# 64-byte operand starts, a start without GpSimd, output weights through gate buffers, and the first FFN weights between two norms

## The chip, the cores and the metric

The kernel runs on one core of a Trainium2 chip, in one launch, on one token sequence of 1024 positions with a model width of 1024. The time is the device time of one execution in microseconds (us), the median of the runs. PE is TensorE, DVE is VectorE, ACT is ScalarE, POOL is GpSimd and SP is SyncE, which issues the transfers.

## The reference, cut to what matters

```python
h = rmsnorm(x, norm_mix_pre)
q_a, f_a, i_a, g_a, q_b, k_b, v_b, gate_raw = split(h @ w_in)
y_a = hgrn2_mix(q_a, f_a, i_a, g_a, lb, hg_out_norm)         # 4 heads of 128, chunks of 64
y_b = diff_attention(q_b, k_b, v_b, lam, lam_init, da_subln)  # 4 heads, two softmaxes each
gate_a, gate_b = split(sigmoid(gate_raw))
merged = gate_a * (y_a @ w_up_a) + gate_b * (y_b @ w_up_b)
x = x + rmsnorm(merged @ w_out, norm_mix_post)
h = rmsnorm(x, norm_ffn_pre)
ff = silu(h @ w_ffn_gate) * (h @ w_ffn_up)                    # width 2816
x = x + rmsnorm(ff @ w_ffn_down, norm_ffn_post)
```

Everything is in float32; x is 1024 x 1024.

## The kernel before, in words

**Split operands.** Each float32 operand of a large product is cut into a high and a low half, and a product of two such operands is three matmuls (high with high, high with low, low with high) into one PSUM bank. The high half is a copy or cast on ACT, the low half a subtraction on DVE or POOL (`split`, L633 to L635). A matmul takes 128 rows by 512 columns.

**Stages.** (1) The input, transposed, arrives in eight tiles `xr`; ACT and DVE cut each into `act` halves (L270, L271), while PE begins the first two projections, `f0` and `q0`, tile by tile as they come. The weights of the projections come through `w_raw`, `w_hi` and `w_lo`, three buffers each (`fetch_w`, `split_w`); the constant `ON_DVE` says for which weights DVE makes the low half (L110), POOL makes the others. The squares of the input for the first norm (L284 on POOL for the first three tiles, L286 on ACT for the others) are summed on DVE, and `column_rstd` makes the statistics from them. (2) Four HGRN heads, then four attention heads, each woven with the remaining projections as filler: before a head, `next(filler)` puts a few steps of a gate projection (six matmuls each) on PE; then the head's first scores (L547) follow, whose operands `atw` DVE makes. (3) The up-projection: for each of eight column blocks j, two products with L143, L144 and L146, whose banks DVE multiplies by the gates (L741), adds (L745) and splits. `put_wo` (L718) brings the eight output weights through `w_raw` and splits them: two within the loop over j, on POOL, six behind it, on DVE and POOL in turn. (4) The out-projection (`out_mults`, L850 to L852) in eight row tiles t, with the two norms of `residual` (L798 to L809) behind each, and, `LAG` ticks later, the transposes of `transposed` (L832), which `put_T` (L816 to L820) splits into the FFN's left-hand tiles T. (5) The FFN's gate and up products, 22 units of seven products of 12 matmuls (`GateUp.product`, L950 to L953), each unit's weights loaded by `load_raw` (L887) and cut by `prep` into `hl` or slot tiles; the first two products of four units (`EARLY`) come first, then the rest. (6) `Down` (L1103 to L1106), and the last rows.

**What sets the order.** The program is written stage by stage; the builder's scheduler places the instructions on each engine within their dependencies, and each engine runs its row in order. `after` adds an ordering edge without a wait between engines. A `Ring` hands out buffers in turn; a `Cutter` cuts them from 16 KB slots.

**Where tiles lie.** The constants and the slots lie from the left end of the on-chip memory; the pools with `side="right"` (`wp`, `actp`, `gwp`, two slots and `hl_more`) lie from the right end. Counted from the sizes of the pools, every tile of the right side that PE reads starts at an odd multiple of 32 bytes, and every one of the left at a multiple of 64. T4 lies in a slot of the right side, the other T on the left.

Two places of the code that the rest speaks of:

```python
(dve if len(ws) in ON_DVE else pool).tensor_tensor(out=lo, in0=raw, in1=hi.bitcast(F32), op=ALU.subtract)
...
for _ in range(7):
    next(filler)
weave(attn(h, vs[2 + h // 2], (h % 2) * P), filler, AT_RATIO[h])
...
prepare(min(x + (1 if x < 2 * EARLY else AHEAD), len(seq) + 1))
```

## Time and profile before

| | |
|---|---|
| runs before | 1532.06, 1530.64, 1531.58 us; median 1531.58 |
| the profiled execution | 1532.58 us, of which the span of its records is 1530.7 |
| granted clock of PE, mean | 0.992 |
| PE busy | 1499.1 us of the span |
| DVE, ACT, POOL busy | 884.3, 604.8, 528.3 us |
| transfers | 189.44 MB, mean 124 GB/s |

The profile is of one execution. Busy times of the engines lie beside one another; a granted clock of 1.00 means that PE ran at its full 2.4 GHz, and the other level, 1.2 GHz, pulls the mean of a stretch below that. A matmul's duration in a record is longer than its distance to the next, since they are pipelined; the pace is the distance between two starts. "Idle before" in a row is time in which that engine had nothing running ahead of the instruction, with the instruction that released it.

### The profile page before, as it was taken

To read this page: it belongs to the slowest core of one execution; us is meant where nothing else is said; L and a number is where in the kernel's file an instruction comes from. 1 tells how busy PE (TensorE), PEld (TensorE's weight loads), DVE (VectorE), ACT (ScalarE), POOL (GpSimd) and SP (SyncE) were. 2 spreads that over 40 slices of the span, in tenths; PEclk is the share of its full clock that TensorE was granted. 3 is DMA by queue.
4 is the path that set the end of the run, shared out by engine and by line. 5 is a ranking of instruction groups with operands and counts; after the bars stand their busy time and mean duration, and the time that the engine had idled before them with its cause. 6 is when DMAs were issued, how large, how long until landed. Compare 5 with 4: busy or idle time off the path is not lost. (4 is left out here: it accounts for less than half of the span.)

```text
span 1530.7 us, 19524 instructions
## 1 busy us (share of the span) xinstructions
PE 1499.1 (98%) x7334; PEld 1255.9 (82%) x7334; DVE 884.3 (58%) x1596; ACT 604.8 (40%) x1138; POOL 528.3 (35%) x347
## 2 busy tenths in 40 slices
PE   8999999999999999999999999999999999999998
PEld 6988988989878888888877778888888888888886
DVE  8667387354474646554325777555555544477744
ACT  5422323225344343554325554444444444423211
POOL 4211111231221313124601265455555444456600
PEclk9999999999999999999999999999999999999999
DMA  5101021021121211174323336444444435977333
GB/s 218 56 28 55 15 70 42 31 81 41 56 69 56 69 70 55 56 287 159 117 85 122 110 98 241 157 152 151 151 151 149 146 109 191 377 283 259 138 130 118
DMA packets 53231, 189.44 MB, mean 124 GB/s; under 512 B 6032, under 2 KB 6160, under 8 KB 53136
## 3 DMA queue, kind: packets, MB, share of 16 engines
q1 hardware_dynamic: 53136, 188.18, 34.4%
q8 instruction: 58, 0.95, 0.2%
q14 instruction: 37, 0.30, 0.1%
HBM read 131.54 MB, written 56.62 MB: 123 GB/s over the span
## 5 line engine op out<-in xcount | busy, mean ns | idle before, releaser
L635 POOL TENSOR_TENSOR slot<-slot 128x512 fp32r<-128x512 f32 x166 | 228.7, 1388 | 190.6 <-ACT slot L634 190.0
L110 POOL TENSOR_TENSOR w_lo<-w_raw,w_hi 128x1024 fp32r<-128x1024 f32 x50 | 123.1, 2464 | 479.5 <-ACT w_hi L108 458.5
L634 ACT CAST slot<-slot 128x512 fp32r<-128x512 f32 x252 | 151.3, 620 | 227.9 <-PE mbank L952 48.8
L143 PE MATMUL gbank<-act,w_hi 128*128 128x512 f32 x560 | 225.7, 403 | 1.6 <-ACT act L270 1.5
L144 PE MATMUL gbank<-act,w_hi 128*128 128x512 f32 x560 | 220.8, 394 | 3.9 <-DVE act L271 3.9
L906 DVE TENSOR_TENSOR slot<-slot 128x512 f32<-128x512 f32 x120 | 107.1, 895 | 143.8 <-POOL slot L635 87.5
L146 PE MATMUL gbank<-act,w_lo 128*128 128x512 f32 x560 | 175.2, 392 | 0.0
L635 POOL TENSOR_TENSOR hl<-slot,hl 128x512 fp32r<-128x512 f32 x70 | 96.8, 1389 | 97.4 <-ACT hl L634 96.8
L144 PEld LDWEIGHTS gbank<-act,w_hi 128*128 128x128 f32 x560 | 105.5, 188 | 23.9 <-DVE act L271 4.9
L146 PEld LDWEIGHTS gbank<-act,w_lo 128*128 128x128 f32 x560 | 105.4, 188 | 22.6
L143 PEld LDWEIGHTS gbank<-act,w_hi 128*128 128x128 f32 x560 | 105.3, 188 | 21.4 <-ACT act L270 2.1
L108 ACT CAST w_hi<-w_raw 128x1024 fp32r<-128x1024 f32 x52 | 54.5, 1047 | 121.9 <-issue 68.7
L950 PE MATMUL gbank<-slot 128*128 128x512 f32 x232 | 92.2, 397 | 3.0 <-ACT slot L634 3.0
L953 PE MATMUL gbank<-slot 128*128 128x512 f32 x232 | 91.9, 396 | 0.6 <-POOL slot L635 0.6
L952 PE MATMUL gbank<-slot 128*128 128x512 f32 x232 | 91.9, 396 | 0.0
L558 ACT ACTIVATE s<-s,nm 128x128 f32<-128x128 f32 (+7 forms) x64 | 49.2, 769 | 86.0 <-DVE nm L556 86.0
L634 ACT CAST hl<-slot 128x512 fp32r<-128x512 f32 x70 | 43.3, 621 | 90.1 <-PE mbank L952 24.0
L237 PE MATMUL gbank<-w_hi,act 128*128 128x256 f32 x256 | 73.8, 288 | 0.0
L238 PE MATMUL gbank<-w_lo,act 128*128 128x256 f32 x256 | 72.8, 284 | 0.0
L239 PE MATMUL gbank<-w_hi,act 128*128 128x256 f32 x256 | 72.7, 284 | 0.0
L950 PE MATMUL mbank<-slot 128*128 128x512 f32 x176 | 69.2, 393 | 2.4 <-ACT slot L957 2.4
L953 PE MATMUL mbank<-slot 128*128 128x512 f32 x176 | 69.3, 394 | 0.0
(261 smaller groups left out, 3489.3 us busy)
## 6 DMA issues: line engine op xcount, KB each, us to landing
t<-slot SPq DMA_DIRECT2D x68, 512.0 KB, 3.3
slot<-t SPq DMA_DIRECT2D x68, 512.0 KB, 6.7
slot<-w_gu SPq DMA_DIRECT2D x48, 512.0 KB, 4.1
w_raw<-w_proj SPq DMA_DIRECT2D x36, 512.0 KB, 3.6
slot<-w_down SPq DMA_DIRECT2D x22, 512.0 KB, 4.8
g<-gw SPq DMA_DIRECT2D x16, 512.0 KB, 2.6
slot<-g SPq DMA_DIRECT2D x16, 512.0 KB, 4.7
xr<-xT SPq DMA_DIRECT2D x8, 512.0 KB, 8.2
```

What stands on the lines that cost most here:

```text
L110: (dve if len(ws) in ON_DVE else pool).tensor_tensor(out=lo, in0=raw, in1=hi.bitcast(F32), op=ALU.subtract)
L143: pe.matmul(ps, lhsT=hi[:, kw, :], rhs=rhs(ka, b, 0), start=first and i == 0, stop=False)
L144: pe.matmul(ps, lhsT=hi[:, kw, :], rhs=rhs(ka, b, 1), start=False, stop=False)
L146: pe.matmul(ps, lhsT=lo[:, kw, :], rhs=rhs(ka, b, 0), start=False, stop=last and i == n - 1)
L237: pe.matmul(ps[:, :256], lhsT=a[:, 0, :], rhs=hi[:, kt % 4, :], start=kt == 0, stop=False)
L238: pe.matmul(ps[:, :256], lhsT=a[:, 0, :], rhs=lo[:, kt % 4, :], start=False, stop=False)
L634: copied = act.copy(out=dst[:, 0], in_=src)
L635: eng.tensor_tensor(out=dst[:, 1], in0=src, in1=dst.bitcast(F32)[:, 0], op=ALU.subtract)
L906: dve.tensor_tensor(out=t, in0=a, in1=b, op=op)
L950: pe.matmul(ps, lhsT=hl[:, 0, w], rhs=t[:, 0, c, :], start=not on and c == 0, stop=False, skip_group_check=on)
L952: pe.matmul(ps, lhsT=hl[:, 0, w], rhs=t[:, 1, c, :], start=False, stop=False, skip_group_check=on)
L953: pe.matmul(ps, lhsT=hl[:, 1, w], rhs=t[:, 0, c, :], start=False, stop=c == 3, skip_group_check=on)
```

## The change

Five things, in the order of the program:

1. A tile of 32 bytes (`pad`) is put at the right end, so that every pool of the right side moves by 32 bytes.
2. While the input is split, POOL gets no work: the low half of weight 0 goes to DVE (`ON_DVE` with 0), and all eight squares go to ACT, behind its splits.
3. Before each attention head eight instead of seven steps of the filler are put on PE.
4. `put_wo` takes its raw buffer from the `tmp` ring, in which the gates were, and copies with ACT; the low halves on DVE from the third weight on come behind the last merged branch (`m_last`).
5. `residual` is a generator that stops between its two norms. Unit 0 is prepared behind row tile 6, unit 1 between the two norms of row tile 7; the out-projection's code stands behind the units for that. The lag of the transposes is one tick shorter from t = 4 on. `put_T` reads the copy in SBUF and not the bank. `prep` splits on DVE until product 16, then on POOL, and in the first eight products it is called one product earlier.

```diff
@@ -42,7 +42,7 @@
 PAIRS = 2 * CHUNKS
 ROWS = range(2 * PAIRS, NF)
 STEPS = (2, 8, 32)
-ON_DVE = (1, 4)
+ON_DVE = (0, 1, 4)
 NMASK = 1 + 3 * len(STEPS)
 HG_YIELD = (3, 2, 3)
 V_PRE, V_HG, V_DA, V_LB = 0, 8, 9, 10
@@ -56,6 +56,7 @@
 
     const = ctx.enter_context(tc.tile_pool(name="const", bufs=1))
     small = ctx.enter_context(tc.tile_pool(name="small", bufs=3))
+    ctx.enter_context(tc.tile_pool(name="pad", bufs=1, side="right")).tile([P, 8], F32, name="pad")
     old = ctx.enter_context(ExitStack())
     wp = old.enter_context(tc.tile_pool(name="wp", bufs=3, side="right"))
     hts = ctx.enter_context(ExitStack())
@@ -280,10 +281,7 @@
             next(f0)
             next(q0)
             sq = sqs if kt == 0 else start.tile([P, S], F32, name="sq", bufs=3)
-            if kt < 3:
-                pool.tensor_tensor(out=sq, in0=xrs[kt], in1=xrs[kt], op=ALU.mult)
-            else:
-                after(act.activation(out=sq, in_=xrs[kt], func=AF.Square), h_last, "the squares follow the splits")
+            after(act.activation(out=sq, in_=xrs[kt], func=AF.Square), h_last, "the squares follow the splits")
             if kt:
                 after(dve.tensor_tensor(out=sqs, in0=sqs, in1=sq, op=ALU.add), l_last, "the squares follow the splits")
         run(f0)
@@ -691,7 +689,7 @@
         if h + 1 < NH:
             todo.append(project(13 + h, partial(put_q, h + 1)))
         filler = chain(*todo)
-        for _ in range(7):
+        for _ in range(KT):
             next(filler)
         weave(attn(h, vs[2 + h // 2], (h % 2) * P), filler, AT_RATIO[h])
         if h + 1 == NH:
@@ -716,10 +714,13 @@
     wo = []
 
     def put_wo(eng):
-        raw = wp.tile([P, 1024], F32, name="w_raw")
+        raw = tmp.take()
         sp.dma_start(out=raw, in_=w_out[len(wo)])
         t = two(w_cut.take())
-        split(t, raw, eng)
+        act.copy(out=t[:, 0], in_=raw)
+        lo = eng.tensor_tensor(out=t[:, 1], in0=raw, in1=t.bitcast(F32)[:, 0], op=ALU.subtract)
+        if len(wo) >= WO_AHEAD and eng is dve:
+            after(lo, m_last, "the merged branches go first")
         wo.append(t)
 
     up_a = [(k, k) for k in range(4)]
@@ -744,7 +745,9 @@
             cs = slice(n * HALF, (n + 1) * HALF)
             dve.tensor_tensor(out=gs[0][:, cs], in0=gs[0][:, cs], in1=gs[1][:, cs], op=ALU.add)
             t = two(m_cuts[n].take())
-            split(t, gs[0][:, cs], dve if j == KT - 1 else pool)
+            act.copy(out=t[:, 0], in_=gs[0][:, cs])
+            m_last = (dve if j == KT - 1 else pool).tensor_tensor(out=t[:, 1], in0=gs[0][:, cs],
+                                                                  in1=t.bitcast(F32)[:, 0], op=ALU.subtract)
             row.append(t)
         mT.append(row)
         if j >= KT - WO_AHEAD:
@@ -798,6 +801,7 @@
             act.activation(out=h[:, cs], in_=ps, func=AF.Square, scale=1.0 / 32.0, accum_out=ss[:, d:d + 1])
             dve.tensor_tensor(out=ag[:, cs], in0=ps, in1=gpost[:, cs], op=ALU.mult)
         r = rstd(ss)
+        yield
         dve.scalar_tensor_tensor(out=x, in0=ag, scalar=r, in1=x, op0=ALU.mult, op1=ALU.add)
         sp.dma_start(out=x2_dram[t], in_=x)
         s2 = small.tile([P, 1], F32, name="ss1")
@@ -812,12 +816,12 @@
     def four(a):
         return a.rearrange("p (k c) -> p k c", c=P)
 
-    def put_T(i, b, src, eng, lo_src=None):
+    def put_T(i, b, src, eng):
 
         blk = slice(b * P, (b + 1) * P)
         t = T[i]
         act.copy(out=t[:, 0, :, blk], in_=four(src))
-        eng.tensor_tensor(out=t[:, 1, :, blk], in0=four(src if lo_src is None else lo_src),
+        eng.tensor_tensor(out=t[:, 1, :, blk], in0=four(src),
                           in1=t.bitcast(F32)[:, 0, :, blk], op=ALU.subtract)
 
     def transposed(t):
@@ -834,7 +838,7 @@
         if t < 4:
             for g, pt in enumerate(pts):
                 act.copy(out=f[:, g, :], in_=pt)
-                put_T(1 + g, b, f[:, g, :], dve, pt)
+                put_T(1 + g, b, f[:, g, :], dve)
             return
         a = fs[b]
         act.copy(out=f[:, 1, :], in_=pts[1])
@@ -860,26 +864,8 @@
         while due and due[0][1] <= 0:
             transposed(due.pop(0)[0])
 
-    load_x(0)
-    load_x(1)
...
-        residual(t, ps)
-        load_x(t + 2)
-        due.append([t, LAG])
-
-
+
+    prep_eng = [dve]
     raw_ring, hl_ring, sum_ring = Ring([raw0]), Ring([hl_more.tile([P, S], F32, name="hl") for _ in range(2)]), Ring([])
 
     def load_raw(src, ring=raw_ring):
@@ -925,7 +911,7 @@
             else:
                 src = self.sum(q(0, 1), self.s[6], ALU.subtract)
             t = two(hl_ring.take())
-            split(t, src)
+            split(t, src, prep_eng[0])
             self.hl[i] = t
 
     t2_dram = [[dram.tile([P, 2, HALF], F32, name=f"t2_{p}_{i}") for i in range(8)] for p in range(NF // 2)]
@@ -1005,15 +991,39 @@
         yield
 
     units = [GateUp(f) for f in range(NF)]
-    units[0].prep(1)
-    units[0].prep(2)
-    for i in (6, 3, 7):
-        new_T(i, 0)
...
+    load_x(0)
+    load_x(1)
...
+        rest = residual(t, ps)
+        next(rest)
+        if t == 7:
+            for i in (6, 3, 7):
+                new_T(i, 0)
+            raw_ring.parts = cuts(slot(1), S)
+            hl_ring.parts += cuts(slot(1), S)
+            mixed = slot(1)
+            sum_ring.parts = cuts(mixed, HALF, 0, 3 * HALF)
+            ev.parts = cuts(mixed, HALF, 3 * HALF) + cuts(slot(2), HALF)
+            units[1].prep(1)
+            units[1].prep(2)
+        run(rest)
+        load_x(t + 2)
+        due.append([t, LAG - (t >= 4)])
+        if t == 6:
+            units[0].prep(1)
+            units[0].prep(2)
 
     def late_T():
         while due:
@@ -1064,7 +1074,9 @@
             unit.prep(i)
 
     for x, (u, i) in enumerate(seq):
-        prepare(min(x + (1 if x < 2 * EARLY else AHEAD), len(seq) + 1))
+        prepare(min(x + (2 if x < 2 * EARLY else AHEAD), len(seq) + 1))
+        if x == 4 * EARLY:
+            prep_eng[0] = pool
         if x < 2 * EARLY and i == 2:
             units[u].raw = [None, None]
         if side and next(side[0], "end") == "end":
```

What this does to the order, at three places. First PE, at the first attention head: `act` are the input's halves, `atw` the operands of the scores, `gbank` the gate projection's banks. Before:

```order
L146 MATMUL gbank_2811<-act_190,w_lo_2736 128x512
L146 MATMUL gbank_2812<-act_193,w_lo_2736 128x512
L547 MATMUL mbank_2860<-atw_2793,atw_2728 128x256
L547 MATMUL mbank_2860<-atw_2794,atw_2728 128x256
L547 MATMUL mbank_2870<-atw_2799,atw_2731 128x256
L547 MATMUL mbank_2870<-atw_2800,atw_2731 128x256
L143 MATMUL gbank_2811<-act_198,w_hi_2734 128x512
L144 MATMUL gbank_2811<-act_198,w_hi_2734 128x512
L143 MATMUL gbank_2812<-act_201,w_hi_2734 128x512
L144 MATMUL gbank_2812<-act_201,w_hi_2734 128x512
```

and after the change:

```order
L147 MATMUL gbank_2815<-act_194,w_lo_2740 128x512
L147 MATMUL gbank_2816<-act_197,w_lo_2740 128x512
L144 MATMUL gbank_2815<-act_202,w_hi_2738 128x512
L145 MATMUL gbank_2815<-act_202,w_hi_2738 128x512
L144 MATMUL gbank_2816<-act_205,w_hi_2738 128x512
L145 MATMUL gbank_2816<-act_205,w_hi_2738 128x512
L147 MATMUL gbank_2815<-act_202,w_lo_2740 128x512
L147 MATMUL gbank_2816<-act_205,w_lo_2740 128x512
L545 MATMUL mbank_2874<-atw_2797,atw_2732 128x256
L545 MATMUL mbank_2874<-atw_2798,atw_2732 128x256
L545 MATMUL mbank_2884<-atw_2803,atw_2735 128x256
L545 MATMUL mbank_2884<-atw_2804,atw_2735 128x256
```

The six matmuls of the last input tile, which stood behind the four score matmuls, now stand ahead of them.

Second DVE, where the up-projection ends: L741 (L742 after) are the multiplies of banks by gates, L635 of 128x1024 (L721 after) the low halves of output weights. Before:

```order
L745 TENSOR_TENSOR slot_5873<-slot_5873 128x512 x2
L635 TENSOR_TENSOR slot_6606<-w_raw_6609,slot_6606 128x1024
L741 TENSOR_TENSOR slot_5873<-slot_5873,gbank_6529 128x512
L741 TENSOR_TENSOR slot_5873<-slot_5873,gbank_6530 128x512
L635 TENSOR_TENSOR slot_6615<-w_raw_6618,slot_6615 128x1024
L741 TENSOR_TENSOR slot_5873<-slot_5873,gbank_6557 128x512
L741 TENSOR_TENSOR slot_5873<-slot_5873,gbank_6558 128x512
L745 TENSOR_TENSOR slot_5873<-slot_5873 128x512 x2
L635 TENSOR_TENSOR slot_6371<-slot_5873,slot_6371 128x512
L635 TENSOR_TENSOR slot_6375<-slot_5873,slot_6375 128x512
```

and after the change:

```order
L746 TENSOR_TENSOR slot_5883<-slot_5883 128x512 x2
L742 TENSOR_TENSOR slot_5883<-slot_5883,gbank_6532 128x512
L742 TENSOR_TENSOR slot_5883<-slot_5883,gbank_6533 128x512
L742 TENSOR_TENSOR slot_5882<-slot_5882,gbank_6560 128x512
L742 TENSOR_TENSOR slot_5882<-slot_5882,gbank_6561 128x512
L746 TENSOR_TENSOR slot_5883<-slot_5883,slot_5882 128x512 x2
L749 TENSOR_TENSOR slot_6375<-slot_5883,slot_6375 128x512
L749 TENSOR_TENSOR slot_6379<-slot_5883,slot_6379 128x512
L721 TENSOR_TENSOR slot_6598<-slot_5882,slot_6598 128x1024
L721 TENSOR_TENSOR slot_6605<-slot_5883,slot_6605 128x1024
L721 TENSOR_TENSOR slot_6612<-slot_5883,slot_6612 128x1024
```

The weights' low halves stood between the multiplies; now they stand behind the merged branches' halves (L749).

Third ACT, at the start of the FFN: L804 and L809 (L808 and L813 after) are the second norm of row tile 7, L634 (L632 after) the casts of FFN weights, L819 (L823 after) those of T. Before:

```order
L819 CAST slot_7426<-slot_7116 128x4x128
L819 CAST slot_7424<-slot_6862 128x4x128
L957 COPY slot_7429<-gbank_7431 128x512
L819 CAST slot_7426<-slot_7116 128x4x128
L804 ACTIVATE slot_6640,ss1_7320<-slot_6639 128x1024
L634 CAST slot_7428<-slot_7427 128x512
L960 ACT_TABLE_LOAD
L960 ACTIVATE slot_7429<-slot_7429 128x512
L809 ACTIVATE slot_6639<-slot_6639,r1_7325 128x512 x2
L634 CAST slot_7428<-slot_7427 128x512
```

and after the change:

```order
L823 CAST slot_7409<-slot_6948 128x4x128
L632 CAST slot_7413<-slot_7412 128x512 x2
L823 CAST slot_7409<-slot_6948 128x4x128
L823 CAST slot_7410<-slot_7190 128x4x128 x2
L844 COPY slot_7190<-mbank_7376 128x512
L823 CAST slot_7048<-slot_7190 128x4x128
L632 CAST slot_7413<-slot_7412 128x512 x2
L801 ACTIVATE slot_6635,ss2_7400<-gbank_7333 128x512
L823 CAST slot_7409<-slot_6948 128x4x128
L801 ACTIVATE slot_6635,ss2_7400<-mbank_7334 128x512
```

The casts of the weights stood behind the last second norm (L804, L809); now four of them stand ahead of the row tile's first norm (L801).

## Rows read from the trace of the kernel before

**Rows 1.** The page: busy time of each engine (us, share of the span, instructions).

```profile
PE 1499.1 (98%) x7334; PEld 1255.9 (82%) x7334; DVE 884.3 (58%) x1596; ACT 604.8 (40%) x1138; POOL 528.3 (35%) x347
```

**Rows 2.** Stretches: us, PE, PEld, DVE, ACT, POOL busy (count), PEclk, DMA share, GB/s.

```profile
20.00:35.00 15.00, 15.00 (x68) 12.43 (x67) 14.80 (x18) 5.40 (x6) 2.73 (x1) 1.00 0.27 90
690.00:750.00 60.00, 60.00 (x258) 48.24 (x257) 23.02 (x34) 26.42 (x32) 31.01 (x19) 1.00 0.41 142
764.00:775.00 11.00, 8.79 (x32) 6.74 (x31) 4.92 (x7) 2.27 (x3) 0.28 (x1) 0.84 0.65 239
815.00:830.00 15.00, 12.86 (x53) 10.09 (x52) 8.95 (x13) 10.63 (x21) 1.62 (x3) 0.89 0.34 120
866.00:910.00 44.00, 38.01 (x152) 29.74 (x151) 33.87 (x40) 26.49 (x48) 28.25 (x20) 0.88 0.32 108
```

**Rows 3.** Timeline of PE in Down: start us, us, operation, count, idle before.

```profile
1308.87 0.40 PE L1103 MATMUL mbank<-hl,slot 128*128 128x512 f32 x1
...
1314.48 0.40 PE L1103 MATMUL gbank<-slot 128*128 128x512 f32 x1
...
1325.40 0.40 PE L1103 MATMUL gbank<-hl,slot 128*128 128x512 f32 x1
```

**Rows 4.** Groups by line: busy us, mean ns, idle before (PE, mixed pairs).

```profile
L143 PE MATMUL gbank<-slot,w_hi 128*128 128x512 f32 x128 | 50.7, 396 | 0.0
...
L950 PE MATMUL gbank<-slot,hl 128*128 128x512 f32 x120 | 47.3, 394 | 0.0
...
L950 PE MATMUL mbank<-slot,hl 128*128 128x512 f32 x88 | 34.9, 397 | 0.0
...
L1103 PE MATMUL gbank<-hl,slot 128*128 128x512 f32 x40 | 15.8, 394 | 0.0
...
L1103 PE MATMUL mbank<-hl,slot 128*128 128x512 f32 x32 | 12.6, 394 | 0.0
```

**Rows 5.** Timeline of DVE while the input is split.

```profile
7.13 4.24 DVE L271 SCALAR_TENSOR_TENSOR act<-xr,vec,act 128x512 fp32r<-128x512 f32 x2 [3.42 <-ACT act L270]
...
23.86 3.39 DVE L271 SCALAR_TENSOR_TENSOR act<-xr,vec,act 128x512 fp32r<-128x512 f32 x5
```

**Rows 6.** Timeline of POOL in the same stretch (two squares).

```profile
10.79 5.17 POOL L284 TENSOR_TENSOR sq<-xr 128x1024 f32<-128x1024 f32 x2
```

**Rows 7.** Timeline of PE where the first two projections end.

```profile
35.51 0.28 PE L237 MATMUL gbank<-w_hi,act 128*128 128x256 f32 x1
```

**Rows 8.** Line L547 (attention scores): idle us of PE before it, times.

```profile
  DVE atw L524: 3.6, 4
  DVE atw L522: 0.9, 4
```

**Rows 9.** Timelines of PE, DVE and ACT where the up-projection ends.

```profile
765.78 0.39 PE L852 MATMUL gbank<-slot 128*128 128x512 f32 x1
768.38 0.52 PE L850 MATMUL gbank<-slot 128*128 128x512 f32 x1 [2.21 <-DVE slot L741]
...
769.12 0.63 PE L852 MATMUL gbank<-slot 128*128 128x512 f32 x1
769.54 0.63 PE L850 MATMUL gbank<-slot 128*128 128x512 f32 x1
...
766.50 1.23 DVE L635 TENSOR_TENSOR slot<-w_raw,slot 128x1024 fp32r<-128x1024 f32 x1 [5.63 <-ACT slot L634]
767.64 1.28 DVE L741 TENSOR_TENSOR slot<-slot,gbank 128x512 f32<-128x512 f32 x2
...
765.42 1.05 ACT L634 CAST slot<-w_raw 128x1024 fp32r<-128x1024 f32 x1 [5.15 <-DMA w_raw<-w_out]
```

**Rows 10.** Timeline of PE in the out-projection, its transposes.

```profile
820.84 0.66 PE L832 MATMUL mbank<-ident,slot 128*128 128x128 f32 x4 [1.13 <-DVE slot L820]
```

**Rows 11.** Timeline of PE at the start of the FFN.

```profile
875.09 0.80 PE L950 MATMUL gbank<-slot 128*128 128x512 f32 x1 [3.01 <-ACT slot L634]
...
904.06 0.50 PE L950 MATMUL mbank<-slot 128*128 128x512 f32 x1 [2.36 <-ACT slot L957]
```

More of the change, by code (lines that the diff above doesn't have):

```diff
@@ L861, in tick @@
             transposed(due.pop(0)[0])
-    load_x(0)
-    load_x(1)
-    lefts = [gbank() for _ in range(4)]
-    for k in range(KT):
-        for t in range(4):
-            out_mults(lefts[t], k, t, 0)
-    for t in range(8):
-        if t == 4:
-            new_T(5, 1)
-        ps = [lefts[t] if t < 4 else gbank(), mbank()]
-        for k in range(KT):
-            for d in range(2 if t >= 4 else 1):
-                out_mults(ps[-1] if t < 4 else ps[d], k, t, 1 if t < 4 else d)
-            if k % (4 if t < 4 else 2) == (3 if t < 4 else 1):
-                tick()
-        residual(t, ps)
-        load_x(t + 2)
-        due.append([t, LAG])
+    prep_eng = [dve]
     raw_ring, hl_ring, sum_ring = Ring([raw0]), Ring([hl_more.tile([P, S], F32, name="hl") for _ in range(2)]), Ring([])
@@ L1007, in block_kernel @@
     units = [GateUp(f) for f in range(NF)]
-    units[0].prep(1)
-    units[0].prep(2)
-    for i in (6, 3, 7):
-        new_T(i, 0)
-    raw_ring.parts = cuts(slot(1), S)
-    hl_ring.parts += cuts(slot(1), S)
-    mixed = slot(1)
-    sum_ring.parts = cuts(mixed, HALF, 0, 3 * HALF)
-    ev.parts = cuts(mixed, HALF, 3 * HALF) + cuts(slot(2), HALF)
+    load_x(0)
+    load_x(1)
+    lefts = [gbank() for _ in range(4)]
+    for k in range(KT):
+        for t in range(4):
+            out_mults(lefts[t], k, t, 0)
+    for t in range(8):
+        if t == 4:
+            new_T(5, 1)
+        ps = [lefts[t] if t < 4 else gbank(), mbank()]
+        for k in range(KT):
+            for d in range(2 if t >= 4 else 1):
+                out_mults(ps[-1] if t < 4 else ps[d], k, t, 1 if t < 4 else d)
+            if k % (4 if t < 4 else 2) == (3 if t < 4 else 1):
+                tick()
+        rest = residual(t, ps)
[16 more added lines that the diff above has]
+            units[0].prep(2)
     def late_T():
```

## The prediction

> **What bounds the kernel now.** First the page's busy times: PE is busy for 1499.1 of 1530.7 us [rows 1]. A gain must therefore shorten PE's own work, or remove one of the few places where PE waits; time saved on DVE, ACT or POOL counts only where PE waits for it. Next a table of stretches, for PE's busy time and the granted clock [rows 2]: in most of them PE is full and the clock is 1.00, but 764 to 775 us has 8.79 of 11.00 us busy at 0.84, 815 to 830 has 12.86 of 15.00 at 0.89, and 866 to 910 has 38.01 of 44.00 at 0.88. Then, for each such place, the timelines of PE and of the engine that released it. The profiled execution took 1532.58 us, 1.0 above the median of 1531.58, and the sum below is made against it. A measurement of this kernel can tell about 0.2%, 3 us, from no change.
>
> **The pace of a matmul.** In the Down stage, with every buffer ready, 24 matmuls that read hl start between 1308.87 and 1314.48, one per 234 ns; the next 48, with both operands in slot, take until 1325.40, one per 227.5 ns [rows 3]. Shape, clock and stage are the same. From the sizes of the pools, hl starts at an odd multiple of 32 bytes and slot (left side) at a multiple of 64; act, w_hi and w_lo lie as hl does. A matmul lasts 0.40 us in the records [rows 3], so a stretch counts those of 0.40 us more: from 690 to 750, where w_hi and w_lo meet slot, 60.4 us / 258 = 234 ns; from 20 to 35, where they meet act, 15.4 / 68 = 226 ns [rows 2]. Two odd starts cost nothing, then, and two even ones nothing; the price is one of mixed starts, 6.5 to 7.5 ns a matmul.
>
> **Alignment.** The pad moves everything on the right side by 32 bytes; every 512-wide operand is then at a multiple of 64. Mixed now: 3 x 128 of the up-projection, 3 x (120 + 88) of gate and up, 3 x (40 + 32) of Down, 1224 in all [rows 4]. T4 also lies on the right: by the program 96 of the gate/up products pair it with hl (not mixed) and 168 pair it with slot (mixed), so 1296. At 7 ns that is 9.1 us, all of it on PE's path. Bounds: 0, if the pace hangs on something else that hl and w_hi share (the right side itself, for one), and 9.7 at 7.5 ns. I take 9.1, since two stages with different neighbours show the same two paces.
>
> **Start of the program.** While POOL runs, a 128x512 operation of DVE takes 2.12 us (4.24 for two at 7.13); when POOL is idle it takes 0.68 (3.39 for five at 23.86) [rows 5]. POOL's work then is one half of a weight split and three squares, the last two in 5.17 us [rows 6]. The change gives the squares to ACT and the split to DVE, and POOL is silent until 19 us or so. DVE's first weight half costs 1.2 us (as a 128x1024 operation does elsewhere [rows 9]), then each half of an activation 0.68, so PE runs without a gap from about 8.7 us. The two projections are 96 matmuls of 0.227 us, 21.8 us: they end at 30.5, against 35.51 now [rows 7], 5.0 earlier. The squares end earlier too, but the statistics behind them (sums, POOL's power, DVE's diagonal) now have less PE work in front of them; I give 1.0 back. Net 4.0, bounds 2.5 and 6. A rule can be weighed here. The Trainium skill ("SBUF — State Buffer", "SBUF: two separate sides") says that a DVE operation with two SBUF inputs and a GpSimd operation that reads SBUF exclude each other for the whole instruction. By that rule alone DVE gets back what the three squares last, 7.5 us, and the term would be 7.5 less 1.0; the rows agree that DVE waits (2.12 against 0.68), but PE's own 21.8 us caps the gain below that.
>
> **Attention.** At each of four heads PE idles before the first scores, 0.9 us for one operand and 3.6 for the other over the four heads, 4.5 in all [rows 8]. With `range(KT)` six more matmuls, 1.36 us, stand ahead of the first scores (first order listing). They are moved, not added; the weave behind has six fewer, and the matmuls that cover the end of a head are as many as before. 4 x 1.13 to 4 x 1.36: I take 5.0, bounds 3 and 5.4.
>
> **Between up- and out-projection.** PE has a matmul at 765.78 and the next at 768.38, with 2.21 us idle, for a bank that L741 on DVE must release at 767.64. L741 stands behind L635 of an output weight (766.50), that behind ACT's cast (765.42), and that waited 5.15 us for a transfer into w_raw [rows 9]. Behind it the clock is for a time at the lower of its two levels, 1.2 GHz, with a matmul every 0.42 us (769.12 to 769.54 [rows 9]): 0.16 x 11 = 1.8 us more [rows 2]. After the change the weights land in the eight buffers of the tmp ring, and on DVE all multiplies and the merged branches stand ahead of the weights' low halves (second order listing). 4.0 go; bounds 2.5 and 4.2. What comes next is DVE's first weight: from the end of the up-projection at 764.6 (five matmuls before 765.78), six operations of 0.64 us (1.28 for two [rows 9]) and one of 1.23 make 769.7, and PE wants it three steps of 12 matmuls in, at 772.8.
>
> **Out-projection.** PE idles 2.1 us from 815 to 830 [rows 2], in two groups of transposes that wait for a bank which L820 on DVE still reads, the first for 1.13 us [rows 10], and the clock pays 0.11 x 15 = 1.6 us. L824 now reads the copy in SBUF, so ACT's copy alone frees the bank, two DVE operations earlier. 3.5 of 3.8, bounds 1 and 4.
>
> **Start of the FFN.** PE idles 6.0 us between 866 and 910 and the lower clock costs 0.12 x 44 = 5.3, together 11.3 [rows 2]. The two large waits are 3.01 us at 875.09, for a split that ACT's order has behind the last norm (third order listing, before), and 2.36 us at 904.06, for an eviction on ACT [rows 11]. The change loads these weights ahead of the last stores, splits unit 0 right behind the gains, and puts unit 1's casts between two norms (third order listing). Eighteen low halves go from POOL to DVE, 0.68 each, and take POOL's operations out of DVE's way. From 866 to 910 DVE is busy 33.87 of 44 us [rows 2], part of that stretched by POOL. LAG one shorter for t of 4 and up brings transposes 12 matmuls (2.7 us) forward, which leaves no slack for the chain of a norm: 0 to 0.5 us at each of three. I take 9.5, bounds 5 and 11.3.
>
> **Sum.** 9.1 + 4.0 + 5.0 + 4.0 + 3.5 + 9.5 = 35.1; 1532.6 - 35.1 = 1497.5. Against the median it would be 1496.5; I keep 1497.5. The lower bounds of the gains come to 14.0 (1518.6), the upper to 40.6 (1492.0).
>
> **The rivals.**
>
> Stalls that only move. Each removed wait has something close behind it: the third output weight, the statistics, the norm chains at the FFN's start. If half of the 26 us outside alignment comes back, the time is 1497.5 + 13 = 1510.5. For it: long waits are followed by a slow clock that costs nearly as much (6.0 us idle and 5.3 of clock above), so that one new wait is paid twice. Against it: the order listings put the late work ahead of what PE needs at every one of these places. 0.15.
>
> The pad is worth nothing, because the pace hangs on the side and not on the start. Then the other terms stand: 1497.5 + 9.1 = 1506.6. For it: no row of before has an aligned operand of the right side beside one of the left. Against: two right-side operands together run at 226 ns, so the side alone is not slow. The Trainium skill ("SBUF — State Buffer", "Operand start alignment") asks only for starts at a multiple of the element size, and adds that it speaks of legality and not of speed; by it alone the pad would be worth 0. 0.08.
>
> DVE becomes the bound in the first sixteen products of the FFN, and the kernel is slower. DVE has 33.87 us of work in 44 [rows 2]; the eighteen halves add 12.2, 46.1 in all. If POOL's other work keeps stretching DVE's operations, the products wait for splits, one after another, and PE stays at the lower clock, at 0.42 us a matmul where 0.227 was. The price is 16 products x 12 matmuls x 0.2 = 38 us, in place of the 9.5 saved and of the 5.3 that the slow clock costs already: 1497.5 + 9.5 + 38 - 5.3 = 1539.7. It decides at 12 x 0.227 = 2.72 us of DVE work per product. Against it: a good part of the 33.87 is stretch, and the halves that POOL gives up are what stretches. 0.04.
>
> The change doesn't do what it says: the builder's order leaves the waits as they are. The listings speak against it at three places. Only alignment would be left, 1523.5. 0.02.
>
> **How the numbers follow.** The forecast has 0.71 and the time 1497.5 us. Its own range, from bounds that don't all fail together, is 1490 to 1507. To hold 8 in 10, the range takes in the rival without the pad and most of the moved stalls: 1490 to 1512. Faster by over 0.2%: forecast, moved stalls, no pad and the unchanged order, 0.95; within 0.2%: 0.02, from mixtures of moved stalls and a DVE near its bound; slower: 0.03, most of the DVE case.
>
> **What would show it.** The granted clock at 1.00 and PE full in 764 to 775, 815 to 830 and 866 to 910, shifted by what was saved; one pace in Down, 227 ns for hl and slot alike; no idle time before the scores; the projections of the start done near 30.5 us. The forecast is wrong if hl still runs at 234 ns, if PE waits for DVE at the first products of the FFN, or if a wait of over 2 us shows up at a new place, with a slow clock behind it.

## The result, and the profile after

The changed kernel takes 1506.47 us (median of 4 runs, 1505.85 to 1507.01) against 1531.82 for the kernel before, measured beside it: a ratio of 0.9839, with a 95% interval of 0.9827 to 0.9852. That is 25.4 us faster. The forecast was 1497.5 us with a range of 1490 to 1512: the direction and the range hold, but the time is 9 us above the forecast.

The page of the changed kernel, its busy times:

```profile
PE 1489.4 (99%) x7334; PEld 1252.1 (83%) x7334; DVE 877.2 (58%) x1617; ACT 607.8 (40%) x1141; POOL 487.8 (32%) x323
```

PE's busy time fell by 9.7 us against [rows 1], and its idle time, which is the span less that, from 31.6 to 15.5 us. So most of the gain is idle time that is gone, and of PE's own work less went than the 9.1 of alignment and the 8.7 of slow clock (1.8 + 1.6 + 5.3) would make together.

The stretches that answer to [rows 2], in the same columns:

```profile
8.00:30.00 22.00, 22.00 (x100) 17.88 (x99) 20.23 (x27) 19.73 (x27) 3.38 (x2) 1.00 0.74 284
680.00:740.00 60.00, 60.00 (x259) 48.11 (x258) 28.41 (x32) 23.99 (x28) 30.04 (x18) 1.00 0.42 140
752.00:764.00 12.00, 12.00 (x54) 9.88 (x53) 8.19 (x9) 2.98 (x4) 4.58 (x2) 1.00 0.70 237
800.00:820.00 20.00, 18.25 (x88) 14.64 (x87) 13.43 (x21) 14.41 (x30) 2.16 (x4) 1.00 0.35 131
849.00:890.00 41.00, 38.87 (x166) 31.34 (x165) 37.26 (x57) 26.20 (x49) 5.17 (x5) 0.96 0.28 90
```

PE is full in the first 22 us of real work, and from 752 to 764, where it had been at 8.79 of 11.00. From 800 to 820 it still idles 1.75 us, but the clock is at 1.00. From 849 to 890 it idles 2.1 us, and 0.04 x 41 = 1.6 us go to the clock. From 680 to 740, where w_hi and w_lo meet slot, there are 259 matmuls, one more than before: with (60 + 0.40) / 259 = 233 ns, the price that the pad should have removed is still paid. Down says the same, and a little more. The timeline of PE there, with start and duration in front:

```profile
1283.88 0.40 PE L1115 MATMUL mbank<-hl,slot 128*128 128x512 f32 x1
...
1289.39 0.40 PE L1115 MATMUL gbank<-slot 128*128 128x512 f32 x1
...
1300.32 0.40 PE L1115 MATMUL gbank<-hl,slot 128*128 128x512 f32 x1
```

The 24 matmuls that read hl now come every 229.6 ns (234 before [rows 3]), the 48 behind them every 227.7.

The waits of PE that remain in the changed kernel, those of the first heads and of the very start left out (us in total, times, the longest):

```profile
PE mbank L836 <- ACT slot L813: 3.5, 2, 2.1
...
PE gbank L239 <- POOL w_lo L111: 0.9, 1, 0.9
...
PE mbank L836 <- ACT slot L840: 0.4, 1, 0.4
```

The waits of [rows 8], [rows 9] and [rows 11] are gone, and of those in [rows 10] 0.4 us is left, for ACT's copy. New is a wait of the last transposes of a group for the norm ahead of them (L813), twice:

```profile
812.49 1.27 PE L836 MATMUL mbank<-ident,slot 128*128 128x128 f32 x8 [1.35 <-ACT slot L813]
...
859.62 1.27 PE L836 MATMUL mbank<-ident,slot 128*128 128x128 f32 x8 [2.13 <-ACT slot L813]
```

### The profile page after: what moved, and what is told of

Read it like the earlier page. It is cut to its first block, busy times and chain, and to the rows that moved or that the text cites. A ratio compares the mean times of both kernels' runs of the same rounds, so it can differ in the third digit from the quotient of the medians.

```text
span 1504.9 us, 19508 instructions
## 1 busy us (share of the span) xinstructions
PE 1489.4 (99%) x7334; PEld 1252.1 (83%) x7334; DVE 877.2 (58%) x1617; ACT 607.8 (40%) x1141; POOL 487.8 (32%) x323
## 4 chain that ended last, share of the span: by engine, by line
PE 94%; DVE 3%; ACT 1%; issue 1%; POOL 0%; DMA 0%; DVEq 0%; POOLq 0%; SPq 0%; ACTq 0%
PE gbank L145 10%; PE gbank L144 10%; PE gbank L147 10%; PE gbank L936 5%; PE gbank L939 5%; PE gbank L938 5%; PE mbank L939 4%; PE mbank L936 4%; PE mbank L938 4%; PE mbank L382 3%; PE mbank L545 2%; PE mbank L587 2%; PE gbank L239 2%; PE gbank L240 2%; PE gbank L238 2%; PE gbank L1115 2%
## 5 line engine op out<-in xcount | busy, mean ns | idle before, releaser
L111 POOL TENSOR_TENSOR w_lo<-w_raw,w_hi 128x1024 fp32r<-128x1024 f32 x49 | 119.9, 2451 | 461.0 <-ACT w_hi L109 433.3
L633 POOL TENSOR_TENSOR slot<-slot 128x512 fp32r<-128x512 f32 x140 | 192.7, 1386 | 174.0 <-ACT slot L632 173.9
L632 ACT CAST slot<-slot 128x512 fp32r<-128x512 f32 x236 | 141.9, 621 | 209.7 <-PE mbank L938 45.8
L892 DVE TENSOR_TENSOR slot<-slot 128x512 f32<-128x512 f32 x120 | 102.3, 854 | 137.8 <-POOL slot L633 87.6
L633 POOL TENSOR_TENSOR hl<-slot,hl 128x512 fp32r<-128x512 f32 x62 | 85.0, 1376 | 81.2 <-ACT hl L632 76.2
L936 PE MATMUL gbank<-slot 128*128 128x512 f32 x232 | 90.9, 392 | 0.0
L939 PE MATMUL gbank<-slot 128*128 128x512 f32 x232 | 90.7, 391 | 0.0
L938 PE MATMUL gbank<-slot 128*128 128x512 f32 x232 | 90.5, 390 | 0.0
L632 ACT CAST hl<-slot 128x512 fp32r<-128x512 f32 x70 | 43.4, 621 | 86.3 <-PE mbank L938 23.6
L548 DVE CUSTOM_DVE_ANT_0 s<-mbank,alibi 128x512 f32<-128x512 f32 (+3 forms) x96 | 49.5, 553 | 41.3 <-PE mbank L545 41.3
L633 DVE TENSOR_TENSOR slot<-slot 128x512 fp32r<-128x512 f32 x96 | 68.2, 740 | 8.9 <-ACT slot L632 8.2
L936 PE MATMUL mbank<-slot 128*128 128x512 f32 x176 | 69.4, 394 | 0.0
```

What stands on the lines that cost most here:

```text
L632: copied = act.copy(out=dst[:, 0], in_=src)
L633: eng.tensor_tensor(out=dst[:, 1], in0=src, in1=dst.bitcast(F32)[:, 0], op=ALU.subtract)
L936: pe.matmul(ps, lhsT=hl[:, 0, w], rhs=t[:, 0, c, :], start=not on and c == 0, stop=False, skip_group_check=on)
L938: pe.matmul(ps, lhsT=hl[:, 0, w], rhs=t[:, 1, c, :], start=False, stop=False, skip_group_check=on)
L939: pe.matmul(ps, lhsT=hl[:, 1, w], rhs=t[:, 0, c, :], start=False, stop=c == 3, skip_group_check=on)
```

## The experiments

Twelve kernels were run, in three groups, each beside the kernel before on the same chip; its medians there were 1531.16, 1531.67 and 1531.59 us. Stage lengths are taken from the timelines, from a stage's first matmul to the next one's.

### The pad: none, 96, 352 and 224 bytes

After the result, the question was what the 234 ns had hung on. By the pools' sizes, hl lies 352 bytes (modulo 512) from a slot before the change, 320 after it, 256 with a pad of 96 bytes, 0 with one of 352, and 128 with one of 224.

```diff
-    ctx.enter_context(tc.tile_pool(name="pad", bufs=1, side="right")).tile([P, 8], F32, name="pad")
```

> The changed kernel without the pad: its right side lies as in the kernel before, 352 bytes (modulo 512) from the slots, an odd multiple of 32. In the changed kernel the pad gave about 1.8 us and not 9.1: the up-projection went from 89.95 to 89.60 us, Down from 154.28 to 153.45. If the pad alone did that: 1508.3 us, up-projection 89.9 to 90.0 us (234 ns a matmul), Down 154.3. If those small gains came from elsewhere (fewer stores or splits beside): 1506.5, and 89.6 and 153.45 stay.

```diff
-    ctx.enter_context(tc.tile_pool(name="pad", bufs=1, side="right")).tile([P, 8], F32, name="pad")
+    ctx.enter_context(tc.tile_pool(name="pad", bufs=1, side="right")).tile([P, 24], F32, name="pad")
```

> The changed kernel with a pad of 96 bytes in place of 32: right and left tiles are then a multiple of 256 bytes apart, not only of 64. Theory A, the price hangs on the distance of the two operands of a matmul modulo a larger power of two: up-projection at 227 ns (384 x 6.4 = 2.5 us less, 87.1 us), gate and up 3.5 us less, Down 0.4 less, 1500 us in all. Theory B, the price hangs on one operand being on the right side and the other on the left, and the start plays a small part: within 1 us of the changed kernel, 1505.5 to 1507.5, up-projection 89 to 90 us.

The next has 88 elements in place of 24:

> A pad of 352 bytes: right and left tiles are a multiple of 512 bytes apart. Theory A with a period of 128 or 256 bytes: as with 96 bytes, 1500 us. Theory A with a period of 512: this one reaches 1500 and 87.1 us for the up-projection while 96 bytes does so only in part. Theory B: 1505.5 to 1507.5, as the changed kernel.

and the last 56:

> The changed kernel with a pad of 224 bytes: right and left tiles are an odd multiple of 128 bytes apart (256 with the pad of 96, 512 with 352, an odd multiple of 64 with 32, of 32 with none). If the period is 128 bytes: up-projection 87.0 us, Down 152.3, about 1498.5 us in all. If it is 256: the up-projection between 87.2 and 89.6 us, and 1500 to 1506 us in all.

Measured: 1510.62 us with no pad (ratio to before 0.9866, interval 0.9851 to 0.9881), 1506.47 with 32 bytes, 1498.48 with 96 (0.9788, 0.9774 to 0.9803), 1498.50 with 352 (0.9786, 0.9770 to 0.9802), and 1505.97 with 224 (one run). The stretch from 680 to 740, first with no pad (the count of matmuls is in brackets behind PE's busy time),

```profile
680.00:740.00 60.00, 60.00 (x257) 48.22 (x256) 29.83 (x31) 26.24 (x32) 33.56 (x19) 1.00 0.44 153
```

then with 96 bytes,

```profile
680.00:740.00 60.00, 60.00 (x267) 49.67 (x266) 26.37 (x33) 23.82 (x28) 29.29 (x18) 1.00 0.41 141
```

and with 224:

```profile
680.00:740.00 60.00, 60.00 (x259) 48.28 (x258) 28.49 (x32) 24.37 (x29) 30.51 (x18) 1.00 0.43 142
```

257, 267 and 259 matmuls: only the pad of 96 removes the price. In Down, with 96 bytes and then with 224:

```profile
1276.63 0.39 PE L1115 MATMUL mbank<-hl,slot 128*128 128x512 f32 x1
...
1282.07 0.39 PE L1115 MATMUL gbank<-slot 128*128 128x512 f32 x1
...
1292.95 0.39 PE L1115 MATMUL gbank<-hl,slot 128*128 128x512 f32 x1
```

```profile
1282.81 0.40 PE L1115 MATMUL mbank<-hl,slot 128*128 128x512 f32 x1
...
1288.40 0.39 PE L1115 MATMUL gbank<-slot 128*128 128x512 f32 x1
...
1299.30 0.40 PE L1115 MATMUL gbank<-hl,slot 128*128 128x512 f32 x1
```

With 96 bytes both kinds come every 226.7 ns; with 224, hl's come every 233. The pad of 352 gives the same lengths as the one of 96: 87.04 us for the up-projection (89.95 before), 152.32 for Down (154.28 before). So, with the distances counted from the pools' sizes, the price is gone at 256 and at 0 bytes (modulo 512) and paid at the three others tried, 352, 320 and 128: a multiple of 64 or of 128 is not enough. Theory A stands, with a period of 256 bytes; theory B (one side against the other) falls. A pad of 32 takes 234 to 233 ns where w_hi meets slot and to 229.6 where hl meets slot in Down. The kernel with no pad is 4.1 us slower than the changed one, which is more than the stages show: 0.35 in the up-projection, 0.83 in Down and 0.7 in gate and up. In the profiles the rest lies ahead of the first scores (335.08 against 332.09): the projections end 0.7 us later, from 30 to 50 us the granted clock is 0.83 in place of 0.91 (1.6 us), and PE waits 0.8 us for the statistics. The end of this stretch varies among kernels with the pad of 32 too, from 332.1 to 334.4, and two of them also show 0.83; whether the pad plays a role there was not tried apart.

### The lag of the transposes

```diff
-        due.append([t, LAG - (t >= 4)])
+        due.append([t, LAG])
```

> The changed kernel with the lag of all transposes at 4 ticks, as before. The changed kernel waits 2.13 us at 859.6 for the last row tile's second norm (ACT L813) ahead of its transposes. Theory: the shorter lag makes that wait; 12 matmuls (2.7 us) more stand in front of them now, so the wait and the slow clock behind it (1.6 us) go: 1503 us. Rival: the later transposes only move the wait to the first product that needs their T tiles: 1506 to 1507, with a wait on DVE or ACT between 860 and 880.

Measured: 1506.38 us, as the changed kernel (1506.47). The theory falls; the rival is right in the time, though not in the place: the wait before the last transposes is as long as it was, only later.

```profile
862.87 1.27 PE L836 MATMUL mbank<-ident,slot 128*128 128x128 f32 x8 [2.15 <-ACT slot L813]
```

The reason is in DVE's timeline. In the changed kernel:

```profile
850.38 0.68 DVE L848 TENSOR_TENSOR slot<-slot 128x512 f32<-128x512 f32 x1
...
851.58 0.68 DVE L802 TENSOR_TENSOR slot<-gbank,slot 128x512 f32<-128x512 f32 x1
...
854.01 2.31 DVE L805 SCALAR_TENSOR_TENSOR slot<-slot,r 128x1024 f32<-128x1024 f32 x1 [0.43 <-POOL r L785]
```

and in the kernel with the longer lag:

```profile
850.23 0.69 DVE L802 TENSOR_TENSOR slot<-gbank,slot 128x512 f32<-128x512 f32 x1 [0.17 <-ACT slot L801]
850.84 0.68 DVE L845 TENSOR_TENSOR slot<-mbank,slot 128x512 f32<-128x512 f32 x1
...
853.23 1.79 DVE L848 TENSOR_TENSOR slot<-slot 128x512 f32<-128x512 f32 x1
854.94 0.68 DVE L849 TENSOR_TENSOR slot<-slot,mbank 128x512 f32<-128x512 f32 x1
...
856.78 2.30 DVE L805 SCALAR_TENSOR_TENSOR slot<-slot,r 128x1024 f32<-128x1024 f32 x1 [0.43 <-POOL r L785]
...
859.60 1.21 DVE L809 TENSOR_TENSOR slot<-slot 128x1024 f32<-128x1024 f32 x1
```

L802, L805 and L809 belong to the two norms of row tile 7, for which PE waits. In the second kernel the work on tile 6's transposes (L845 to L849) has moved too, into the middle of tile 7's first norm, and L805 starts 2.8 us later, about the 2.7 us of matmuls that were put in front of PE's wait. L805 takes 2.3 us in both, where it took 1.28 us at 808.32 in the changed kernel; POOL's L824 runs beside it from 853.95.

If so, tile 6 should stay early and tile 7 alone be late. This kernel does that, with tile 3 a tick later too, on top of the pad of 96 bytes:

```diff
-        due.append([t, LAG - (t >= 4)])
+        due.append([t, LAG + (t == 3) - (4 <= t < 7)])
```

> The kernel with the pad of 96 bytes, and a lag of 5 ticks for row tile 3, 3 for tiles 4 to 6 and 4 for tile 7. With the lag at 4 for all, the wait before the last transposes stayed (2.15 us), since the transposes of tile 6 moved too and their DVE work then stood ahead of tile 7's norm. Theory: with tile 6 left early, tile 7's norm ends as it does now (first half about 0.8 us after the earlier end of the wait) while PE has 2.7 us more to do, so both the wait at tile 7 (2.5 us, and 1.6 us of clock) and the one at tile 3 (1.5 us) go: 1493 us against 1498.5 with the pad alone. Rival: DVE has no spare time there, and the wait turns up at the next product: 1496 to 1498.

Measured: 1495.74 us (0.9769 of before, 0.9754 to 0.9783), 2.7 us less than with the pad alone. Both waits for L813 are nearly gone, but 1.3 us come back some 25 us later (884.05), at a product that waits for DVE:

```profile
PE gbank L936 <- DVE slot L948: 1.3, 1, 1.3
PE mbank L836 <- ACT slot L813: 0.6, 2, 0.4
```

So theory and rival each hold in part: half of the expected 5.5 us is there. Much of it is clock: from 840 to 884 us the granted clock is 1.00, and 0.96 with the pad alone (1.8 us). As the last section shows, this clock does not follow the wait in every kernel. No other kernel of the study is faster than this one.

### The squares at the start

```diff
-            after(act.activation(out=sq, in_=xrs[kt], func=AF.Square), h_last, "the squares follow the splits")
+            if kt < 3:
+                pool.tensor_tensor(out=sq, in0=xrs[kt], in1=xrs[kt], op=ALU.mult)
+            else:
+                after(act.activation(out=sq, in_=xrs[kt], func=AF.Square), h_last, "the squares follow the splits")
```

> The changed kernel with the first three squares back on POOL; the first weight's low half stays on DVE. The changed kernel's first two projections end at 29.5 us, 6.0 earlier than before. Theory by the exclusion of DVE and POOL: three squares of 2.34 to 2.6 us lock DVE's splits again, and 4 to 5 us of the 6 come back: projections end at 33.5 to 34.5 us, 1510.5 us in all. Rival, that the split of weight 0 on DVE was what counted: projections end at 30 to 31 us, 1507 us.

Measured: 1509.22 us, 2.75 above the changed kernel; the two projections end at 34.70 us in place of 29.51. DVE in this kernel,

```profile
7.19 4.68 DVE L272 SCALAR_TENSOR_TENSOR act<-xr,vec,act 128x512 fp32r<-128x512 f32 x2
11.79 2.91 DVE L111 TENSOR_TENSOR w_lo<-w_raw,w_hi 128x1024 fp32r<-128x1024 f32 x1
```

and in the changed one:

```profile
7.00 1.41 DVE L272 SCALAR_TENSOR_TENSOR act<-xr,vec,act 128x512 fp32r<-128x512 f32 x2
8.61 1.23 DVE L111 TENSOR_TENSOR w_lo<-w_raw,w_hi 128x1024 fp32r<-128x1024 f32 x1 [0.21 <-ACT w_hi L109]
9.76 9.36 DVE L272 SCALAR_TENSOR_TENSOR act<-xr,vec,act 128x512 fp32r<-128x512 f32 x14
```

The same two operations take 4.68 us beside the squares and 1.41 without them, and a weight's low half 2.91 and 1.23. So the squares make up 5.2 of the 6.0 us that the projections gained, which is the theory. From 8 to 30 us PE pays in two ways, with 2.5 us of idle time and with a granted clock of 0.84 where the changed kernel has 1.00 (3.5 us):

```profile
8.00:30.00 22.00, 19.49 (x75) 14.92 (x75) 22.00 (x23) 13.71 (x20) 13.40 (x4) 0.84 0.67 251
```

Of the 5.2, 1.2 are given back behind the projections, where from 30 to 50 us the clock is 1.00 and not 0.91: the first scores start at 336.10 and not at 332.09. The Trainium skill ("SBUF — State Buffer", "SBUF: two separate sides") states that a DVE operation with two SBUF inputs and a GpSimd operation that reads SBUF exclude each other for the whole instruction; these rows agree, with 4.68 us against 1.41.

### The weights' low halves in the FFN

```diff
-    prep_eng = [dve]
+    prep_eng = [pool]
```

> The changed kernel with the low halves of the FFN weights on POOL from the first product on, in the new order. In the changed kernel DVE is busy for 37.3 of 41 us from 849 to 890 and POOL for 5.2. Theory of the prediction: POOL's 1.3 to 1.8 us per half and its exclusion of DVE make the waits, so they come back in part: 4 to 6 us slower, 1511 us, with PE waiting for POOL (slot, L633) and a slow clock. Rival: the order alone gave the gain and DVE was near its bound: 1504 to 1507 us.

Measured: 1513.64 us, 7.2 slower than the changed kernel, where the theory said 4 to 6. In the profiles 6.2 us of it are in gate and up (435.57 against 429.40); the rest lies ahead of the first scores (334.39 against 332.09, with the granted clock at 0.83 and not 0.91 from 30 to 50 us), which the edit does not touch. The wait for the last norm is 5.2 us long:

```profile
PE mbank L836 <- ACT slot L813: 5.2, 1, 5.2
PE gbank L936 <- DVE slot L948: 1.7, 2, 1.0
```

POOL does what DVE was to do, and DVE's operations beside it are stretched. POOL,

```profile
851.02 3.46 POOL L824 TENSOR_TENSOR slot<-slot 128x512 fp32r<-128x512 f32 x2
...
857.61 0.85 POOL L785 TENSOR_TENSOR r<-ms,mhalf 128x1 f32<-128x1 f32 x1 [0.16 <-DVE ms L781]
...
859.68 2.25 POOL L633 TENSOR_TENSOR hl<-slot,hl 128x512 fp32r<-128x512 f32 x1
```

and DVE:

```profile
853.24 1.78 DVE L848 TENSOR_TENSOR slot<-slot 128x512 f32<-128x512 f32 x1
...
855.54 0.68 DVE L802 TENSOR_TENSOR slot<-gbank,slot 128x512 f32<-128x512 f32 x1
...
858.50 2.30 DVE L805 SCALAR_TENSOR_TENSOR slot<-slot,r 128x1024 f32<-128x1024 f32 x1 [0.43 <-POOL r L785]
860.72 1.75 DVE L892 TENSOR_TENSOR slot<-slot 128x512 f32<-128x512 f32 x1
862.40 1.21 DVE L809 TENSOR_TENSOR slot<-slot 128x1024 f32<-128x1024 f32 x1
```

Gate and up begin 2.5 us later here. Beyond that, L805 starts 2.0 us later than in the changed kernel, behind operations of tile 6 such as L848 (1.78 us, and 0.68 there), and L809 3.0 us later, behind a sum for a weight (L892, 1.75 us); the wait is longer by the same 3.0 us (5.18 against 2.13). POOL's power of the norm (L785) is not held up by POOL's own row: POOL is idle 0.16 us ahead of it, for DVE. So PE waits for the norm, not for a split as expected: the place of the wait was missed, and of its two causes the rows of this wait show the exclusion of DVE. The order alone, with the halves on POOL, would have gained little: 435.57 us is 1.6 less than before the change, 0.7 of it alignment.

### Three parts undone one at a time

The low halves of the transposes from the bank again:

```diff
-                put_T(1 + g, b, f[:, g, :], dve)
+                put_T(1 + g, b, f[:, g, :], dve, pt)
```

> The changed kernel, with the transposes' low halves read from the bank again, as before. The out-projection went from 101.6 to 95.8 us with the change, of which 4.0 is the wait at its start. Theory: the bank held by DVE makes the two waits of 1.13 and 1.01 us, so that the second group of transposes waits about 1 us again instead of 0.39, and the stage is 1 to 2 us longer: 1507.5 to 1508.5 us. Rival: the norm chain of these row tiles is the limit, whoever holds the bank, and the waits only change their names: 1506 to 1507, stage 95.5 to 96.3.

Measured: 1508.13 us, with runs from 1506.13 to 1510.80 and so too wide to tell from 1506.47; the stage is 96.30 us long against 95.79. The waits are back on DVE, 2.1 us in all, but the wait of 1.35 us for the norm at tile 3 is gone for it:

```profile
PE mbank L836 <- ACT slot L813: 2.1, 1, 2.1
PE mbank L836 <- DVE slot L824: 2.1, 2, 1.1
```

The length of the stage, 0.5 us more, lies where the rival put it (95.5 to 96.3), the median where the theory put it (1507.5 to 1508.5), and four runs of this width can't decide. What the waits show is that they change their names: these row tiles have 24 matmuls each, and without the wait for the bank PE waits nearly as long for a norm.

Seven steps of the filler:

```diff
-        for _ in range(KT):
+        for _ in range(7):
```

> The changed kernel with seven steps of the filler ahead of each attention head. Theory: the four waits of 1.13 us come back and nothing else changes: the four stretches between heads (the first scores of one to those of the next, the last to the up-projection) are 1.2 to 2.5 us longer each, 1511 to 1512.5 us. Rival: the gain there came from elsewhere (the new place of the filler behind the head): 1506 to 1508.

Measured: 1513.82 us, 7.3 slower. The waits are there again, 4.6 us in all,

```profile
PE mbank L545 <- DVE atw L522: 3.6, 4, 0.9
...
PE mbank L545 <- DVE atw L520: 1.0, 4, 0.3
```

and the four stretches add up to 338.4 us against 331.5, of which 1.4 us are the six matmuls of the first head that now lie inside. So 5.5 us are the heads' own, 5.1 of them idle time. In the profiles the rest, 2.2 us, lies ahead of the first scores, where the granted clock from 30 to 50 us is 0.83 and not 0.91; the edit does not touch that part.

The output weights through w_raw:

```diff
-        raw = tmp.take()
+        raw = wp.tile([P, 1024], F32, name="w_raw")
...
-        if len(wo) >= WO_AHEAD and eng is dve:
+        if False:
```

> The changed kernel, with the output weights through w_raw again and their low halves on DVE not held behind the merged branches. Theory: the wait of 2.2 us between up- and out-projection and the slow clock behind it come back: out-projection 99.5 to 100 us against 95.8, 1510.5 us. Rival: only one of the two (the buffers or the order on DVE) makes the wait, and part of the 4 us comes back: 97 to 98 us, 1508 us. No wait at all, 1506.5, would mean that it went with the earlier parts of the change.

Measured: 1509.70 us, 3.2 slower, and the out-projection 99.92 us long in place of 95.79, as the theory has it:

```profile
PE gbank L854 <- DVE slot L742: 2.2, 1, 2.2
```

The buffers and the order on DVE were undone together, so which of the two makes the wait stays open.

### One more low half on DVE

On top of the kernel with a lag for each tile:

```diff
-ON_DVE = (0, 1, 4)
+ON_DVE = (0, 1, 3, 4)
```

> The kernel with the pad of 96 bytes and a lag for each row tile (1495.7 us), with the low half of weight 3 on DVE too. There the first value product waits 0.9 us at 31 us for POOL's 3.0 us low half, DVE's sum beside it takes 3.17 us where 1.23 is usual, and PE waits 1.6 us at 37 us for the statistics' diagonal. Theory: without POOL both waits shrink, 1.5 to 2.5 us less: 1493.7. Rival: POOL's power of the statistics (1.66 us) is the chain that remains, less than 0.7 us gained: 1495 to 1496.

Measured: 1496.16 us against 1495.74: nothing gained. The wait for the weight is gone, and the one for the statistics grew to 2.1 us, from 1.4 in the kernel it builds on:

```profile
PE mbank L187 <- DVE diag L177: 2.1, 1, 2.1
```

So the rival holds in the time, and what PE then waits for is the chain of the statistics.

## Why the prediction was right in direction and 9 us short

Its way of counting held: PE is the bound, and each gain is a wait or a slow stretch of PE that is gone. By stages, the six moved matmuls of the first head counted with the heads:

| Term | forecast | measured | from |
|---|---|---|---|
| alignment | 9.1 | 1.9 | up-projection 0.35, Down 0.83, gate and up 0.7 (with and without the pad) |
| start of the program | 4.0 | 5.3 | first scores 336.01 to 332.09, and 1.36 moved ahead of them |
| attention | 5.0 | 5.8 | four stretches 338.7 to 331.5, less 1.36 |
| between up- and out-projection | 4.0 | 4.0 | wait of 2.2 and slow clock of 1.8 gone; 4.1 come back with w_raw |
| out-projection | 3.5 | 1.8 | the stage's 5.8 less the 4.0 above |
| start of the FFN | 9.5 | 7.1 | gate and up 437.17 to 429.41, less 0.7 |

The measured terms make 25.9, the difference of the two spans 25.8.

**The step that failed is the reading of the pace: "the price is one of mixed starts".** The rows showed two odd starts at the fast pace and two even ones, and one of each at the slow one. They fit as well with a price on the distance between the two operands: all the fast pairs were whole multiples of 512 bytes apart, all the slow ones 352 bytes more than such a multiple. The prediction took the start modulo 64, since the change spoke of it, and never worked out the distance. With that, 320 bytes after the pad would have been seen to differ from all fast pairs. The size of the term was about right: with a pad of 96 bytes the up-projection gives 2.9 us, Down 2.0 and gate and up 5.5 (430.09 with no pad to 424.58), 10.4 in all against the forecast 9.1 and its bound of 9.7. The rival "the pad is worth nothing" had nearly the right time, 1506.6 for 1506.47, but not the right reason, since it hung the price on the side; its nearness is chance, for the pad gave 1.9 and the other terms 2.0 less than forecast. The Trainium skill ("SBUF — State Buffer", "Operand start alignment") speaks of legality alone; the pace is another matter, as these rows and runs show.

**Start and attention** came out above the forecast by 1.3 and 0.8. At the start the projections ended at 29.51 and not at 30.5, and less was given back by the statistics than assumed. In the heads, a shorter wait within one of them went too: with seven steps it is back, 0.6 us for pT.

**Out-projection and the start of the FFN** gave 1.7 and 2.4 less, by the mechanism of the rival of moved stalls, at a size far below it. Behind the bank there was the norm chain of tile 3 (1.35 us), and behind the splits the norm chain of tile 7 (2.13 us, and 1.6 of clock). The prediction allowed 0 to 0.5 us at each of three chains; it had not seen that the work on tile 6's transposes stands on DVE just ahead of tile 7's chain, and one of POOL's operations beside it. Its own sign of being wrong, a wait of over 2 us at a new place with a slow clock behind it, did come (2.13 us at 859.62). The 1.6 us of clock are those of the profiled execution, whose mean clock was 0.996; the three other runs had 0.998 and times within 0.9 us of it, so this part need not be in each.

**DVE as the bound** did not come: it is busy for 37.26 of 41 us in the stretch, and PE waits there once, not sixteen times. With the halves on POOL instead, the kernel is 7.2 us slower. So taking them from POOL was worth more than it cost, as the prediction argued against this rival. That the time is only 9 us off is in part luck: outside alignment, terms 2.1 us above the forecast and 4.1 below it partly cancel.

## What to carry to other kernels

Where two groups of matmuls of one shape have two paces, work out the distance between their operands as well as their starts: here, a multiple of 256 bytes cost nothing and the three other distances tried 1 to 3%, and a pad of 96 bytes in place of 32 was worth 8 us. When a wait is removed, look for the chain that ends next at the same place; here it was within 1 to 2 us. Giving the waiting engine more to do gained nothing where the same move put other work inside that chain (1506.38 against 1506.47); with that work left where it was, both waits nearly went (0.6 us left). An engine that only helps can cost more than it does: DVE's operations beside POOL's took 1.8 to 3.3 times as long (2.31 us for 1.28, 4.68 for 1.41), so that work was cheaper on a nearly full DVE than on an idle POOL.

## What was not expected of the hardware

The pace of a 128x512 matmul changed with the distance of its operands, counted from the pools' sizes: 234 ns at 352 bytes (modulo 512), 233 and 229.6 at 320, 233 at 128, and 226.7 at 256 and 0, where both pads give the same stage lengths. Why, the runs don't tell: none of them separates the loading of the weights from the reading of the moving operand.

The granted clock does not always fall after the same wait. The stretch from 840 to 884 in the changed kernel, with a wait of 2.13 us in it,

```profile
840.00:884.00 44.00, 41.87 (x184) 33.94 (x183) 37.67 (x57) 30.47 (x56) 6.52 (x7) 0.96 0.43 144
```

and in the kernel with the low halves from the bank, with a wait of 2.13 us at the same transposes:

```profile
840.00:884.00 44.00, 41.87 (x191) 34.12 (x190) 38.57 (x58) 31.22 (x58) 7.93 (x8) 1.00 0.43 144
```

PE is busy for the same time, and the clock is 0.96 in one and 1.00 in the other, which is 1.8 us. Ten kernels have this wait, of 2.1 to 2.3 us: over the same stretch five show 0.96 (the changed one, the pads of none, 96 and 352, the seven steps) and five 1.00 (the longer lag, the squares on POOL, the pad of 224, the low halves from the bank, the output weights through w_raw). The prediction had counted on the lower clock behind each wait of over 2 us; what decides was not tried.
